# The coupling blocks of the 32x32 triangular inverses: from row operations on VectorE to 32x32 matrix products on TensorE

## The chip, the cores and the metric

The kernel runs on one core of a Trainium2 chip. A core has five engines that run side by side: TensorE (PE in the profile, with its weight loads listed as PEld), VectorE (DVE), ScalarE (ACT), GpSimd (POOL) and SyncE (SP), which here only issues DMA transfers. Each engine takes its instructions strictly in the order of its own queue and waits on semaphores for the others. The metric is the device time of one execution in microseconds (us), lower is better.

## The reference

One encoder layer over two sequences, 2048 and 512 tokens of width 1024: RMS norm, one input projection, four mixers of width 256 (a chunked gating MLP, a bidirectional gated DeltaNet, a grouped-query attention, a pooling mixer), each times a SiLU gate, then an output projection and the residual. All inputs and outputs are float32. The change touches the DeltaNet alone, and of it this part, once forward and once over the flipped sequence, for 4 heads:

```python
q, k, v, g, beta = (to_chunks(t) for t in (q, k, v, g, beta))
g = jnp.cumsum(g, axis=-1)
decay = jnp.exp(jnp.where(incl, g[..., :, None] - g[..., None, :], -jnp.inf))
k_beta = k * beta[..., None]
lower = jnp.where(strict, jnp.einsum("bnhid,bnhjd->bnhij", k_beta, k) * decay, 0.0)
eye = jnp.eye(DN_CHUNK, dtype=jnp.float32)
t_mat = lax.linalg.triangular_solve(lower + eye, jnp.broadcast_to(eye, lower.shape),
                                    left_side=True, lower=True, unit_diagonal=True)
u = t_mat @ v_beta
w = t_mat @ (k_beta * jnp.exp(g)[..., None])
# then a scan over the chunks: state -> (out, state), using w, u, q, k and t_mat's products
```

So for each chunk, head and direction a unit triangular matrix has to be inverted before the scan over the chunks may use it. The kernel uses chunks of 128 tokens, so that there are 20 of them (16 and 4), each with 4 heads and 2 directions: 160 matrices of 128x128.

## The kernel before, in words

The work is cut into five blocks of 512 tokens (four of the long sequence, one of the short one). A first phase computes the projection that the DeltaNet needs, its convolution and norms; a second one (`phase2`) computes, in three passes over the blocks, the other projections and gates; a third one (`phase3`) is the attention with the output projection mixed in. Products that must be accurate are made of three float16 products; they have 512 columns and stand at lines 127 and 135 (400 columns at line 400), 3000 in all. I call these the big products. Those of `phase2` are the filler beside which the DeltaNet runs.

`deltanet` runs at a higher priority than `phase2`'s second and third pass, and goes block by block, in the order 0, 3, 1, 2 and then the short sequence's block 4. For each block there are three steps and then the scan:

- `pre`, for each tile of 128 tokens: the decay and the products of the keys (`gp`, `kk` on TensorE, lines 1095 to 1110), the matrices `nl` (VectorE, line 1114) and the intra-chunk matrices. The four 32x32 diagonal blocks of each matrix go by DMA to the DRAM tensor `DG`, one matrix per row.
- `lanes`, once per block: `DG` comes back with one 32x32 block in each of the 128 partitions (`nf`), and each partition inverts its own block (`xf`) by elementwise products and sums along rows on VectorE. A helper `dot` does each step as a multiplication (line 1153) and a sum (line 1154). First the two 16x16 halves of the block are inverted together, 15 steps of growing length. Then the 16x16 block between the halves, `z`, is computed: four steps multiply by the matrix, four more by the second inverse. The result goes to the DRAM tensor `XL`.
- `levels`, for each pair of tiles, so twice per block: the inverses come back from `XL` with the blocks' rows across the partitions (`d32`, line 1179, four transfers per call). Products on TensorE couple 32x32 blocks to 64x64 (`z1p`, `t1p`, `tnp`, lines 1206 to 1217) and those to 128x128 (`z2p`, `t2p`). The first of these use 32x32 parts of the array, four at a time on different rows and columns. Between the products ScalarE moves results out of PSUM. The finished inverse goes as float16 pairs to DRAM.
- `rec` (lines 1256 to 1323), for each tile and direction: the scan itself, 40 steps, which load the finished inverses.

The order on each engine isn't written out: a list scheduler sets it when the program is built, from priorities (the DeltaNet's 3000000, the attention's 2000000, the later passes' 1000000) and its own estimate of when each instruction can run. A changed instruction therefore moves the rows of every engine after it. The tiles of the products in `levels` share two PSUM banks in turn (tag "CE").

## Time and profile before

| | |
|---|---|
| time, median of 3 runs | 1568.18 us (1568.1 to 1571.8) |
| the profiled execution's own time | 1574.01 us |
| its span, first to last instruction | 1572.2 us |
| mean granted TensorE clock | 0.959 |
| busy: PE, DVE, ACT, POOL | 1425.8, 1173.3, 797.0, 546.7 us |
| from the first to the last `z1p` product | 445.9 to 823.1 us |

The page lists busy times by engine, then the span in slices, then groups of instructions by line. "Idle before" is the time an engine stood still just before a group, and what ended it. The granted clock is the share of full speed that the chip let TensorE run at in a stretch. In a view of stretches each engine has its busy time and, in brackets, its number of instructions. Products of 512 columns overlap in TensorE, so the mean duration that the groups give for one is longer than the distance at which they follow each other. A float32 product stands in the trace as two records.

### The profile page before, as it was taken

How to read it: one execution, taken by the hardware profiler on the slowest of the kernel's cores; microseconds unless marked ns; L12 is line 12 of the kernel's file. 1: busy time of each engine (PE TensorE's matmuls, PEld its weight loads, DVE VectorE, ACT ScalarE, POOL GpSimd, SP SyncE). 2: the span in 40 equal slices, each digit the busy share in tenths (PEclk: the TensorE clock that was granted, in tenths of full speed). 3: DMA queues.
4: the chain of work that ended last, by engine and by line, in shares of the span. 5: the costliest groups of instructions: out<-in, count | busy, mean ns of one | idle time of the engine just before them, and what ended most of it. 6: DMA issues, size and time to landing. Idle time of an engine off the chain costs nothing. (4 is left out here: it accounts for less than half of the span.)

```text
span 1572.2 us, 34743 instructions
## 1 busy us (share of the span) xinstructions
PE 1425.8 (91%) x13420; PEld 783.5 (50%) x13420; DVE 1173.3 (75%) x2265; ACT 797.0 (51%) x1655; POOL 546.7 (35%) x646
## 2 busy tenths in 40 slices
PE   6999999988989887987889879998799999999898
PEld 3456555543444443544445435555355555555443
DVE  6338579967969887996957769998877887877611
ACT  5244444545454844554546215565567675576400
POOL 3220220044748643455453435555121221121100
PEclk9999999998899989989999999999799999999999
DMA  9845643556566877657689885644411501414332
GB/s 254 283 168 168 190 151 114 150 194 193 160 186 201 258 234 218 199 171 215 186 259 311 278 255 177 202 139 148 161 48 39 173 34 65 160 33 135 114 128 107
DMA packets 250830, 269.65 MB, mean 172 GB/s; under 512 B 95784, under 2 KB 176680, under 8 KB 250024
## 3 DMA queue, kind: packets, MB, share of 16 engines
q1 hardware_dynamic: 250264, 267.36, 54.1%
q8 instruction: 105, 1.72, 0.4%
q14 instruction: 61, 0.50, 0.1%
q0 software_dynamic: 400, 0.07, 0.1%
HBM read 175.66 MB, written 91.77 MB: 170 GB/s over the span
## 5 line engine op out<-in xcount | busy, mean ns | idle before, releaser
L127 PEld LDWEIGHTS <-w 128*128 128x128 f16 x2280 | 223.5, 101 | 307.5 <-issue 81.8
L127 PE MATMUL accz<-xs,w 128*128 128x512 f16 x960 | 243.7, 402 | 16.8 <-DMA xs<-xs 6.7
L958 PE MATMUL op<-wo,mx 128*128 128x512 f16 x960 | 225.3, 379 | 1.0 <-DVE y L962 1.0
L886 DVE TENSOR_REDUCE mm<-mp 128x1 f32<-128x512 f32 x272 | 179.5, 683 | 52.4 <-PE mp L884 52.1
L916 POOL TENSOR_TENSOR p<-e,p 128x512 f16<-128x512 f32 x68 | 86.7, 1274 | 318.6 <-ACT p L915 283.7
L912 ACT ACTIVATE e<-sp 128x512 f32<-128x512 f32 x272 | 153.4, 596 | 79.3 <-PE sp L910 72.9
L916 DVE TENSOR_TENSOR p<-e,p 128x512 f16<-128x512 f32 x204 | 165.8, 828 | 19.3 <-ACT p L915 19.1
L127 PE MATMUL acc<-xs,w 128*128 128x512 f16 x720 | 162.8, 383 | 3.8 <-POOL xs L291 1.5
L915 ACT ACTIVATE p<-e 128x512 f16<-128x512 f32 x272 | 161.2, 632 | 3.4 <-PE O L921 2.0
L921 PEld LDWEIGHTS <-p 128*128 128x128 f16 x3264 | 128.1, 97 | 55.8 <-DVE p L916 11.2
L921 PE MATMUL O<-vt,p 128*128 128x65 f16 (+1 forms) x3264 | 142.6, 193 | 7.5 <-DVE p L916 5.3
L958 PEld LDWEIGHTS <-mx 128*128 128x128 f16 x960 | 91.3, 98 | 104.4 <-issue 1.8
L884 PE MATMUL mp<-ka,qa 128*128 128x512 f16 x272 | 98.7, 395 | 17.3 <-DVE mm L886 10.6
L909 PE MATMUL sp<-qa,ka 128*128 128x512 f16 x272 | 103.9, 384 | 2.6 <-ACT e L912 1.2
L306 DVE SCALAR_TENSOR_TENSOR cv<-raw,convw,cv 128x512 f32<-128x512 f32 x120 | 88.0, 754 | 21.2 <-POOL raw L382 20.6
L910 PE MATMUL sp<-qb,kb 65*128 65x512 f16 x272 | 100.5, 387 | 1.2 <-ACT qb L894 1.0
L127 PE MATMUL accq<-xs,w 128*128 128x512 f16 x360 | 89.5, 391 | 9.9 <-DMA xs<-xs 7.0
L400 PE MATMUL acct<-wtm,xs 128*128 128x400 f16 x480 | 83.8, 332 | 1.9 <-ACT ba L408 0.9
L1268 POOL TENSOR_TENSOR kd<-kv,kds 128x512 f16<-128x512 f32 x40 | 46.9, 1179 | 108.0 <-PE up L1305 56.0
L291 POOL TENSOR_TENSOR xs<-xt,xs 128x512 f16<-128x512 f32 x36 | 49.1, 1386 | 73.5 <-ACT xs L288 73.2
L962 DVE SCALAR_TENSOR_TENSOR y<-op,xr 128x512 f32<-128x512 f32 x40 | 27.5, 687 | 59.2 <-PE op L958 59.1
L127 PE MATMUL accu<-xs,w 128*128 128x512 f16 x240 | 60.9, 403 | 7.2 <-DVE s L616 7.0
(316 smaller groups left out, 2506.8 us busy)
## 6 DMA issues: line engine op xcount, KB each, us to landing
xs<-xs SPq DMA_DIRECT2D x120, 256.0 KB
kx<-kx SPq DMA_DIRECT2D x80, 256.0 KB
at<-at SPq DMA_DIRECT2D x80, 256.0 KB
tt<-tt SPq DMA_DIRECT2D x80, 256.0 KB
xt<-in_xT SPq DMA_DIRECT2D x40, 256.0 KB
xs<-xs SPq DMA_DIRECT2D x5, 2048.0 KB
kv<-kv SPq DMA_DIRECT2D x40, 256.0 KB
mix<-mixs SPq DMA_DIRECT2D x40, 256.0 KB
```

Source lines behind the costliest of these rows:

```text
L127: mm = self.nc.tensor.matmul(ps, w[:, a, k, :], xk, start=k + i == 0, stop=k == 7 and i == 2)
L306: V.scalar_tensor_tensor(cv, raw[:, ct, i:i + 512], self.convw[:, ct, i:i + 1], cv, op0=ALU.mult, op1=ALU.add)
L400: PE.matmul(acc[:, 0:400], xs[:, a, k, tt * 128:(tt + 1) * 128], w[:, c, k, :], start=n == 0, stop=n == 23)
L884: PE.matmul(mp, qa[:, qt * 128:qt * 128 + 128], KA[h // 2][:, sc * 512:sc * 512 + 512], start=True, stop=True)
L886: V.tensor_reduce(mm[:, qt, sc:sc + 1], mp, axis=AX.X, op=ALU.max)
L909: PE.matmul(sp, KA[kv][:, c], qa, start=True, stop=False)
L910: PE.matmul(sp, KB[kv][:, c], qb, start=False, stop=True)
L912: A.activation(e, sp, AF.Exp)
L915: A.activation(p[:, 0], e, AF.Copy)
L916: (G if st % E8 == 1 else V).tensor_tensor(p[:, 1], e, p[:, 0], op=ALU.subtract)
L921: mm = PE.matmul(O[:, qt, 0:z - a], p[:, w, q], v[:, a:z], start=st == 0 and qt == 0 and i == 0, stop=st == nst - 1 and i == 2, skip_group ...
L958: PE.matmul(op, mix[k][:, a, tt * 128:tt * 128 + 128], wo[k][:, c, n * 512:n * 512 + 512], start=i + j == 0, stop=i == 7 and j == 2)
```

## The change

`lanes` now stops after the two 16x16 halves: the eight steps for `z` are gone, and with them the larger scratch tile. `levels` gets what was in `z` as a level of its own ahead of the others. It loads the inverses of both directions in one transfer (`d32s`, 64 rows of `XL`; `pre` writes the rows of `DG` in another order, so that these 64 rows are together). VectorE transposes all of them (`dT`). Then 64 products of 32x32 by 32x16 on TensorE (`zcp`: 8 matrices, 2 directions, 4 diagonal blocks, each block on its own part of the array's diagonal) multiply the matrices' 32x32 diagonal blocks with one column half of the inverses. ScalarE takes the results out of PSUM for each direction, scaled row by row by 0 or 1 (the new constant `m16`) to keep the rows of one half, into `zcs` and a part of `dT`. 64 more products (`ucp`) multiply with the other half, and VectorE adds the result to the upper right 16x16 quarters in `d32s`. From there the levels are as before. `levels` is called ten times, `lanes` five.

```diff
@@ late_consts @@
+        self.m16 = cp.tile([128, 2], F32, name="m16")
+        nc.sync.dma_start(self.m16, I["m16"])
@@ front @@
-        for x in TTs + Tns:
+        zcs = dp.tile([128, 8, 32], F32, name="zcs")
+        for x in TTs + Tns + [zcs]:
             G.memset(x, 0.0)
@@ pre @@
-                l0 = (t % 4 * 2 + d) * 16
+                l0 = t % 4 // 2 * 64 + d * 32 + t % 2 * 16
                 nc.sync.dma_start(self.DG[t // 4][l0:l0 + 16].rearrange("(u b) (r c) -> (b r) u c", u=4, r=32), dg)
@@ lanes @@
             def dot(out, x, y, shape):
-                tmp = dp.tile([128, 1024], F32, tag="ltmp", name="ltmp", bufs=1)
+                tmp = dp.tile([128, 450], F32, tag="ltmp", name="ltmp", bufs=1)
...
             for i in range(1, 16):
                 dot(xh[:, :, 0:i, i], xh[:, :, 0:i, 0:i], nh[:, :, i:i + 1, 0:i], [128, 2, i, i])
-            z = xt[:, 0:16, 16:32]
-            for k in range(0, 16, 4):
-                dot(z[:, k:k + 4, :], nl[:, 16:32, k:16].unsqueeze(1), xt[:, k:k + 4, k:16].unsqueeze(2), [128, 4, 16, 16 - k])
-            for k in range(12, -4, -4):
-                w = xt[:, 16:20 + k, 16 + k:20 + k].rearrange("p b a -> p a b")
-                dot(z[:, :, k:k + 4], w.unsqueeze(1), z[:, :, 0:k + 4].unsqueeze(2), [128, 16, 4, k + 4])
             nc.sync.dma_start(self.XL[b], xf[:, 0:1024])
@@ levels @@
+            l0 = t % 4 // 2 * 64
+            d32s = dp.tile([128, 2, 8, 32], F32, tag="d32", name="d32", bufs=1)
+            dT = dp.tile([128, 2, 8, 32], F32, tag="dT", name="dT", bufs=1)
+            flat = lambda x: x.rearrange("p d u r -> p (d u r)")
+            nc.sync.dma_start(d32s.rearrange("p d u r -> p (d u) r"),
+                              self.XL[t // 4][l0:l0 + 64].rearrange("(v b) (c r) -> (b c) v r", b=4, c=32))
+            V.transpose(flat(dT), flat(d32s))
+
+            blocks = [slice(B * 32, B * 32 + 32) for B in range(4)]
+            zcp = self.bank("CE", [128, 2, 8, 16], "zcp")
+            for u in range(8):
+                for d in both:
+                    for r in blocks:
+                        PE.matmul(zcp[r, d, u, :], at(d, u, r, r), d32s[r, 1, u, 16:32] if d else dT[r, 0, u, 0:16],
+                                  start=True, stop=True, tile_position=(r.start, r.start))
+            zc = dT[:, 0, :, 16:32]
+            A.activation(zcs[:, :, 0:16], zcp[:, 0], AF.Identity, scale=self.m16[:, 0:1])
+            A.activation(zc, zcp[:, 1], AF.Identity, scale=self.m16[:, 1:2])
+            ucp = self.bank("CE", [128, 2, 8, 16], "ucp")
+            for u in range(8):
+                for d in both:
+                    for r in blocks:
+                        PE.matmul(ucp[r, d, u, :], dT[r, 1, u, :] if d else zcs[r, u, :],
+                                  zc[r, u, :] if d else d32s[r, 0, u, 16:32], start=True, stop=True,
+                                  tile_position=(r.start, r.start))
+            V.tensor_tensor(d32s[:, :, :, 16:32], d32s[:, :, :, 16:32], ucp, op=ALU.add)
             for d in both:
                 TT, Tn = TTs[d], Tns[d]
-                d32 = dp.tile([128, 8, 32], F32, tag=f"d32{d}", name="d32", bufs=1)
-                for j in range(2):
-                    l0 = ((t + j) % 4 * 2 + d) * 16
-                    nc.sync.dma_start(d32[:, j * 4:j * 4 + 4], self.XL[t // 4][l0:l0 + 16].rearrange(
-                        "(u b) (c r) -> (b c) u r", u=4, c=32))
+                d32 = d32s[:, d]
                 if d == 0:
-                    tnd = dp.tile([128, 8, 32], F32, tag="tnd", name="tnd", bufs=1)
+                    tnd = dT[:, 0]
                     V.transpose(tnd.rearrange("p u r -> p (u r)"), d32.rearrange("p u r -> p (u r)"))
```

Lines of the changed kernel are numbered a little differently: 1184 is `zcp`, 1187 and 1188 the two moves out of PSUM, 1193 `ucp`, 1196 the addition, 1177 the new transposition; the steps of `dot` are at 1155 and 1156.

On VectorE, in the second block's `lanes`, the end of the old row operations looked like this (`ltmp` is the scratch tile, `lx` the inverse; the sums with 4x16 and 16x4 results belong to `z`; the other rows are `phase2`'s and the scan's):

```order
L1154 TENSOR_REDUCE lx<-ltmp 128x4x16
L660 SCALAR_TENSOR_TENSOR sg<-sh,pinv,rawp 64x512
L1153 TENSOR_TENSOR ltmp<-lnl,lx 128x256
L1154 TENSOR_REDUCE lx<-ltmp 128x4x16
L1153 TENSOR_TENSOR ltmp<-lx 128x1024
L1154 TENSOR_REDUCE lx<-ltmp 128x16x4
L1309 TENSOR_SCALAR S<-up 128x256
L1153 TENSOR_TENSOR ltmp<-lx 128x768
L723 TENSOR_TENSOR k<-k,rb 128x512
```

In the changed kernel VectorE's row after the last step of the halves (2x15) belongs to the levels of the block before, and the addition of `ucp` stands in the queue with the transpositions behind it:

```order
L1155 TENSOR_TENSOR ltmp<-lx,lnl 128x450
L1119 SCALAR_TENSOR_TENSOR dt<-kk,dt 128x256
L1156 TENSOR_REDUCE lx<-ltmp 128x2x15
L1262 TENSOR_TENSOR tt_5366<-tt_4485,tt_5366 128x1024
L725 TENSOR_TENSOR k<-k,rb 128x512
L1196 TENSOR_TENSOR d_5377<-d_5377,ucp 128x16x16
L1202 STREAM_TRANSPOSE dT<-d_5377 128x256
L1210 STREAM_TRANSPOSE tt_4486<-d_5377 32x8x32 x4
L1321 TENSOR_TENSOR v_5682<-up,v_5682 128x256
```

Sixteen row operations per block have left the queue, and two rows per call of `levels` have come in, the second of which waits for a product of TensorE.

On TensorE the first level of the first block began with `z1p`, right behind the big products of `phase2` (`accq`):

```order
L127 LDWEIGHTS w_1471
L127 MATMUL accq<-xs_4003,w_1471 128x512
L1206 MATMUL z1p<-tnd,nl 32x32
L1206 MATMUL z1p<-d_5119,nl 32x32
L1206 MATMUL z1p<-tnd,nl 32x32
```

Now it begins with `zcp`, and the scheduler lays products of the next block's `pre` (`kk`, line 1113) and of `phase2` (`rb`) in between:

```order
L1184 MATMUL zcp<-dT,nl 32x16 x4
L1184 MATMUL zcp<-d_5088,nl 32x16
L636 LDWEIGHTS rexp_3315
L636 MATMUL rb<-rt_3754,rexp_3315 128x512
L1184 MATMUL zcp<-d_5088,nl 32x16 x3
L1184 MATMUL zcp<-dT,nl 32x16 x4
L1184 MATMUL zcp<-d_5088,nl 32x16 x4
L1184 MATMUL zcp<-dT,nl 32x16 x4
L1184 MATMUL zcp<-d_5088,nl 32x16 x2
L1113 LDWEIGHTS kx
L1113 MATMUL kk<-kx 128x256
```

Counted over the whole order, 1605 of the 3000 big products stood ahead of the first `z1p` and 2541 ahead of the last level's last product; now 1488 stand ahead of the first `zcp` and 2230 ahead of that last product. The last step of the scan had 2991 of them ahead and has 2776 now. The products on 32x32 parts of the array stood in 46 runs without another product in between, and stand in 84.

More of the change, by code (lines that the diff above doesn't have):

```diff
@@ L1140, in lanes @@
             xf = dp.tile([128, 1056], F32, tag="lx", name="lx", bufs=1)
-            sq = lambda t: t[:, 0:1024].rearrange("p (a b) -> p a b", b=32)
             halves = lambda t: t.rearrange("p (h x) -> p h x", x=528)[:, :, 0:512].rearrange(
                 "p h (a b) -> p h a b", b=32)[:, :, :, 0:16]
-            nl, xt, nh, xh = sq(nf), sq(xf), halves(nf), halves(xf)
+            nh, xh = halves(nf), halves(xf)
             nc.sync.dma_start(nf[:, 0:1024], self.DG[b])
@@ L1458, in host_arrays @@
     out["rexp2"] = np.tile(blk[:, 4:6].T, (3, 1))
+    half = (np.arange(128) % 32 >= 16).astype(f4)
+    out["m16"] = np.stack([half, 1 - half], 1)
     out["sel"] = np.tile(np.eye(8, dtype=f4), (3, 1))
```

## The prediction

> **What bounds the kernel now.** I read the page's first part, then the stretches, cut at the first and the last `z1p` product and at the phases, then who waits for whom where TensorE loses time.
>
> ```profile
> PE 1425.8 (91%) x13420; PEld 783.5 (50%) x13420; DVE 1173.3 (75%) x2265; ACT 797.0 (51%) x1655; POOL 546.7 (35%) x646
> L1206 PE MATMUL z1p<-tnd,nl x320: 191/191/258, 445.9 to 823.1; 32*32 32x32 f32 x160
> core 0: us, PE busy (x) PEld busy (x) DVE busy (x) ACT busy (x) POOL busy (x), PEclk, DMA share, GB/s
> 360.00:446.00 86.00, 76.59 (x370) 34.60 (x373) 67.31 (x145) 43.75 (x113) 48.49 (x82) 0.88 0.65 199
> 446.00:823.00 377.00, 319.58 (x3969) 176.54 (x3972) 314.88 (x603) 204.26 (x472) 195.72 (x263) 0.91 0.69 210
> 823.00:1120.00 297.00, 258.47 (x3038) 147.27 (x3027) 242.32 (x430) 142.05 (x277) 142.42 (x140) 0.94 0.67 214
> 1120.00:1505.00 385.00, 373.69 (x3892) 211.78 (x3891) 293.87 (x514) 241.79 (x452) 74.88 (x56) 1.00 0.27 89
> ```
>
> Over the whole span TensorE is the busy engine, and from 1120 us on it is 97% busy at full clock (373.69 of 385). From 360 to 823 us it isn't: busy 396.2 of 463 us (76.59 + 319.58), and at a clock of 0.88 and 0.91. VectorE is busy 382.2 us there, 83%, ScalarE 54%. The time TensorE loses in these two stretches is 463 − 396.2 = 66.8 us of standing still and, at the granted clock, 86 x 0.12 + 377 x 0.09 = 44.2 us of slow running: 111 us. That is what can be won there, and nothing after 1120 us can.
>
> Whom TensorE waits for between the first and the last level:
>
> ```profile
> PE turned L626 <- POOL r L92: 11.2, 5, 3.5
> PE accu L127 <- DVE s L616: 7.0, 3, 4.2
> PE accq L127 <- DMA xs<-xs: 6.6, 7, 1.8
> PE gp L1095 <- DVE dt L1116: 6.2, 3, 3.8
> PE kk L1110 <- ACT dt L1102: 5.6, 3, 4.6
> PE accz L127 <- DVE k L723: 4.4, 1, 4.4
> PE up L1300 <- DMA tt<-tt: 3.4, 2, 2.5
> ```
>
> Of these 44.4 us, 17.6 end on VectorE itself and 11.2 on GpSimd's `r`, whose chain starts with a VectorE operation (line 66); 10.0 are DMA, 5.6 ScalarE. So 28.8 of 44.4, 65%, stand behind VectorE's queue. They are filler products that wait for a PSUM bank or a norm which VectorE has not come to yet.
>
> **What is removed.** The eight steps for `z`, five times: 40 multiplications and 40 sums.
>
> ```profile
> L1153 DVE TENSOR_TENSOR ltmp<-lx 128x1024 f32<-128x1024 f32 (+3 forms) x20 | 29.9, 1496 | 0.2
> L1153 DVE TENSOR_TENSOR ltmp<-lnl,lx 128x1024 f32<-128x1024 f32 (+3 forms) x20 | 19.0, 949 | 0.2
> L1154 DVE TENSOR_REDUCE lx<-ltmp 128x64 f32<-128x1024 f32 x10 | 12.1, 1213 | 0.2
> L1154 DVE TENSOR_REDUCE lx<-ltmp 128x64 f32<-128x768 f32 x10 | 9.5, 948 | 0.1
> L1154 DVE TENSOR_REDUCE lx<-ltmp 128x64 f32<-128x512 f32 x10 | 6.8, 680 | 0.2
> L1154 DVE TENSOR_REDUCE lx<-ltmp 128x64 f32<-128x256 f32 x10 | 4.1, 414 | 0.2
> ```
>
> 29.9 + 19.0 + 12.1 + 9.5 + 6.8 + 4.1 = 81.4 us of VectorE, all inside 360 to 823 us. Per block that is 16.3 us bare, but in the first block it spread over 33 us of wall time among other rows, from here:
>
> ```profile
> 397.54 1.22 DVE L1153 TENSOR_TENSOR ltmp<-lnl,lx 128x1024 f32<-128x1024 f32 x1
> 430.08 0.42 DVE L1154 TENSOR_REDUCE lx<-ltmp 128x64 f32<-128x256 f32 x1
> ```
>
> **What is added.** The nearest rows:
>
> ```profile
> L1183 DVE STREAM_TRANSPOSE tnd<-d 128x256 f32<-128x256 f32 x10 | 4.4, 439 | 10.2 <-DMA d<-xl 10.2
> L1302 DVE TENSOR_TENSOR v<-up,v 128x256 f16<-128x256 f32 x40 | 16.3, 416 | 3.4 <-ACT v L1301 3.4
> L1206 PE MATMUL z1p<-d,nl 32*32 32x32 f32 x320 | 9.3, 203 | 0.4 <-DMA d<-xl 0.3
> L1102 ACT ACTIVATE dt<-gp,lcj 128x128 f32<-128x128 f32 x160 | 44.7, 382 | 10.7 <-PE gp L1099 9.8 <-POOL at L1131 0.5
> core 0: us, PE busy (x), PEclk, DMA share, GB/s
> 440.00:448.00 8.00, 0.75 (x64) 1.00 0.97 252
> 630.00:650.00 20.00, 1.21 (x64) 0.91 0.62 179
> ```
>
> VectorE: a transposition of 128x512, twice the 128x256 one, 0.88 us, and an addition of 128x256 from PSUM, 0.42 us; ten times, 13.0 us. Net VectorE loses 81.4 − 13.0 = 68.4 us. ScalarE: two moves of 128x128 per call, 20 x 0.38 = 7.6 us, on an engine that is 54% busy; they cost the end nothing, and if ScalarE were full it would be those 7.6 us.
>
> TensorE: 20 bursts of 64 products. The last two rows are `z1p` alone, 32 products (64 records) of 32x32 by 32x32, four at a time: 0.75 us at full clock, 1.21 us at a clock of 0.91. The new ones have the same weights and half the columns. From below, if columns are all that counts, a burst is as long as one of `z1p`, 0.75 us; from above, twice the longer, 2.42 us. That makes 15 to 48 us. I take twice the shorter, 1.5 us, **30 us** in all, since the weights to load, one per product, don't get fewer. The Trainium skill, TensorEngine Tiling, Instruction Overhead, says that every matmul carries about 60 cycles, so that one column costs the same as sixty; by the 2.4 GHz of its page TensorE: Matmul & The Clock Gate I estimate from it 25 ns each, 32 us for the 1280. `z1p`'s 0.75 us for 32 products, 23 ns each, agrees in size.
>
> The transfers from `XL`: one per call instead of four, with the same 256 KB. VectorE waited 10.2 us in all for the four (the row of line 1183), TensorE 0.3 us (the row of line 1206): the filler covers the rest. Bounds −10 us, if none of it were waited for, and +10, if the one takes twice as long and the filler doesn't reach; I take 0. One memset and one constant's load stand before 360 us, off the path.
>
> New handoffs: TensorE, ScalarE, TensorE, VectorE, in each call. What queues behind the new addition on VectorE (line 1196) are the transpositions that `z1p` and `t1p` wait for, and then rows of the scan. The old rows for such waits are small: `kk` to `nl`, 80 times:
>
> ```profile
> L1114 DVE SCALAR_TENSOR_TENSOR nl<-kk,dt 128x256 f32<-128x256 f32 x80 | 32.3, 415 | 12.5 <-PE kk L1110 9.6 <-ACT dt L1102 2.7 <-PE z2p L1230 0.2
> ```
>
> 9.6 us for 80, 0.12 us each. 30 handoffs give 4 us; I take **3 us**. A level's chain gets longer by at least 0.88 + 1.5 + 0.76 + 1.5 + 0.42 = 5.1 us, 51 us over ten calls, against 81.4 us bare that leave the chain in `lanes`: it is shorter by 30 us before any queueing, and the order says the same, with 311 big products less ahead of the last level than before (2541 to 2230).
>
> **What the relief gives back.** This is the term that decides. 65% of 111 us is 72 us of TensorE's loss behind VectorE. VectorE's load in these two stretches goes from 382.2 of 463 us (83%) to 313.8 (68%), so its free share about doubles, 17% to 32%. If a wait behind a queue goes with the inverse of the free share, it falls to 0.53 of what it was, 34 us won. If VectorE paced the stretch outright, the stretch would shrink by 68.4 / 0.83 = 82 us. If only the 17.6 us of direct waits fell by half, it would be 9 us. Between 9 and 82 I take **47 us**, above the 34, because a standstill also brings a slow clock with it (in the slice from 425 to 436 us TensorE is held up and the clock falls):
>
> ```profile
> 425.00:436.00 11.00, 8.90 (x35) 3.53 (x35) 7.44 (x13) 3.41 (x10) 7.47 (x21) 0.69 0.72 237
> ```
>
> **Sum:** −47 + 30 + 3 = −14 us, on a span of 1572.2 us: 1558. The profiled execution took 1574.0 us by its own time and the median of the runs is 1568.2; 1568.2 − 14 = **1554 us**.
>
> **Rivals.**
>
> *TensorE's bursts cost more than VectorE's relief brings (slower).* The scan follows the levels at once: the order brings it forward too. VectorE's queue then stays as full as before between the levels, with rows of the scan in place of `z`, and TensorE keeps its waits while it has 20 bursts more. For it: what TensorE waits for are filler's banks and norms, all at lower priority than the DeltaNet, which stay behind whatever the DeltaNet gives VectorE. Against it: these rows are only moved, and are missing later, where VectorE is 82% busy as well (242.32 of 297). Price: relief 10, bursts 30 to 48, handoffs 3: +23 to +41, 1600 us. It decides as soon as the relief is under 33 us. The Trainium skill, TensorEngine Tiling, Key Properties, has a rule that pushes this way: a change of the tiling mode drains TensorE. The order has 38 runs more on 32x32 parts. What a change costs is read here:
>
> ```profile
> 448.58 3.40 PE L135 MATMUL accq<-xs,w 128*128 128x512 f16 x15
> 451.91 0.23 PE L1213 MATMUL t1p<-tt,z 32*32 32x32 f32 x4
> 1504.98 62.60 PE op L958 x290
> ```
>
> Big products follow each other at 62.60 / 290 = 0.216 us, so the last of the 15 started at 448.58 + 14 x 0.216 = 451.60, and the small ones 0.31 us after it: 0.1 us more than a big product's distance. 38 runs with a change at each end are 76 x 0.1 = 8 us by that row, within the 15 to 48. That rule, as a result of its own, is the sum with a drain in full: the 0.23 us of a small product for each change, 17 us, 1571 us; the trace's 0.1 us speaks against it.
>
> *No change.* The relief is about 33 us, by the inverse free share, and pays for bursts and handoffs exactly. 1568 us.
>
> *The chain was the bound (much faster).* VectorE paced the stretch: 82 us less, 30 + 3 more, 1519 us. For it: the whole wall of 33 us that `z` took in the first block. Against it: TensorE is 86% busy there, and after the change it would have to be over 95% busy from 360 to 823 us with its 30 us more; there isn't room for all of it.
>
> **How the numbers follow.** My forecast, 1534 to 1563 us: 0.46. Much faster, below 1534: 0.14. No change, within 0.3% (4.7 us, about what a measurement of this kernel can tell from none), the drain in full counted in here: 0.15. Slower: 0.25. Faster in sum 0.60. The range for 8 in 10 runs from the middle of the much faster case to near the slower one's price: **1526 to 1594 us**; the forecast's own is 1534 to 1563.
>
> **What would show it.** Right: in the stretch from 360 us to the last level, VectorE's share falls to about 70%, TensorE's goes to 90%, the clock rises above 0.93; `turned`, `accu` and `gp` wait less; a burst of `zcp` is 1.2 to 1.8 us; the last level ends 40 to 70 us earlier, and what remains runs as from 1120 us on now. Wrong: bursts over 2 us; new waits at line 1196 or of `ucp` for ScalarE above 0.5 us each; VectorE still above 80% in that stretch; or the earlier end of the levels lost again between them and 1120 us, where the filler that was moved behind them finds VectorE full.

## The result: 2.75% slower, and the profile after

The changed kernel takes 1614.07 us (median of 4 runs, 1604.62 to 1619.35) beside 1569.7 us for the kernel before (4 runs). The ratio is 1.0275, 95% interval 1.0220 to 1.0331. I had forecast 1554, faster. The profiled execution took 1619.35 us, its span is 1617.5 us, the mean granted clock 0.950 (before: 1572.2 and 0.959). Two executions of the experiments below stand far apart from the others of their kernels and are left out of the times, one of e3 (7165 us) and the profiled one of e4 (1823 us, at a granted clock of 0.748).

The first part of the page of the changed kernel:

```profile
PE 1454.6 (90%) x15980; PEld 816.4 (50%) x15980; DVE 1122.9 (69%) x2205; ACT 802.4 (50%) x1675; POOL 521.8 (32%) x647
```

Its stretch from 360 us to the last level product:

```profile
core 0: us, PE busy (x) PEld busy (x) DVE busy (x) ACT busy (x) POOL busy (x), PEclk, DMA share, GB/s
360.00:829.50 469.50, 392.42 (x7101) 229.81 (x7102) 323.15 (x710) 256.66 (x624) 231.07 (x337) 0.88 0.68 202
```

VectorE is relieved: 50.4 us less over the span, 69% of the stretch (323.15 of 469.5). TensorE is no busier for it, 84% (392.42 of 469.5) where I wanted 90%, at a clock of 0.88 where I wanted 0.93. First and last starts of four tiles' products say where the time went. Before:

```profile
L1236 PE MATMUL t2p<-tt,z x320: 218/218/363, 464.9 to 858.8; 64*64 64x64 f32 x160
L1305 PE MATMUL up<-v,kd x480: 189/193/258, 498.2 to 1098.7; 128*128 128x64 f16 x160
L127 PE MATMUL accz<-xs,w x960: 376/379/634, 317.3 to 1089.7; 128*128 128x512 f16 x192
L958 PE MATMUL op<-wo,mx x960: 376/379/390, 1132.0 to 1567.2; 128*128 128x512 f16 x192
```

After:

```profile
L1255 PE MATMUL t2p<-tt,z x320: 218/218/267, 451.0 to 829.6; 64*64 64x64 f32 x160
L1324 PE MATMUL up<-v,kd x480: 189/193/261, 469.3 to 1062.0; 128*128 128x64 f16 x160
L127 PE MATMUL accz<-xs,w x960: 376/379/634, 319.8 to 1159.9; 128*128 128x512 f16 x192
L960 PE MATMUL op<-wo,mx x960: 376/379/631, 1174.8 to 1612.7; 128*128 128x512 f16 x192
```

The levels (`t2p`) end 29 us earlier (I had said 40 to 70), the scan (`up`) 37 us earlier, but the filler (`accz`) ends 70 us later, and the output projection (`op`) starts 43 us later. From there to its last product it takes 435 us before and 438 us after. So nearly all of the 45 us of span is lost ahead of the output projection.

TensorE alone by stretches, the kernel before and then the changed one; the columns are the length, TensorE's busy time, the granted clock, the DMA share and GB/s:

```profile
360.00:600.00 240.00, 205.50 (x1947) 0.89 0.66 203
600.00:880.00 280.00, 240.73 (x2938) 0.93 0.73 227
880.00:1130.00 250.00, 217.12 (x2538) 0.94 0.62 196
```

```profile
360.00:600.00 240.00, 209.39 (x3252) 0.90 0.70 210
600.00:880.00 280.00, 214.49 (x4208) 0.83 0.68 205
880.00:1130.00 250.00, 226.73 (x2216) 0.98 0.62 198
```

I add up in each stretch what TensorE loses, as in the prediction: standing still (length less busy) and running slowly (length times what the clock lacks). From 360 to 600 us it loses 60.9 before and 54.6 after; from 600 to 880 us 58.9 and **113.1**; from 880 to 1130 us 47.9 and 28.3. In the first and the third stretch together it loses 26 us less, in the middle one 54 us more. The balance is 28 us of loss; the other 17 of the 45 us are near what 20 bursts last at full clock (1.26 us each, below, 25 us).

This sum is rough, since standing still at a slow clock counts in both terms. The trace also records each step of the clock. If every moment of TensorE's work is weighted with the clock granted at that moment, its work at full clock is 1371.7 us before and 1394.5 us after, 23 us more; the rest of the span, lost to standing still or to running slowly, is 200.5 us before and 223.0 us after, 22 us more. Together they are the 45 us.

Who is waited for tells what happened. The scan's four products before and after (the number behind the bar is busy time, then the mean, then idle time just before them):

```profile
L1300 PE MATMUL up<-r,tt 128*128 128x64 f16 x480 | 26.5, 200 | 11.5 <-DMA tt<-tt 3.4 <-ACT r L1295 2.7 <-DVE r L1296 2.3
L1288 PE MATMUL up<-s,kx 128*128 128x64 f16 x576 | 24.3, 193 | 2.1 <-ACT s L1283 1.3 <-DVE o L1314 0.5 <-DVE s L1284 0.3
L1305 PE MATMUL up<-v,kd 128*128 128x64 f16 x480 | 19.9, 194 | 0.1
L1312 PE MATMUL up<-v,at 128*128 128x64 f16 x480 | 19.9, 194 | 1.2 <-DVE S L1307 1.1 <-DVE S L1309 0.2
```

```profile
L1307 PE MATMUL up<-s,kx 128*128 128x64 f16 x576 | 27.8, 201 | 24.1 <-DVE o L1333 16.4 <-DVE zz L609 5.7 <-DVE s L1303 2.0
L1319 PE MATMUL up<-r,tt 128*128 128x64 f16 x480 | 26.8, 200 | 23.8 <-DMA tt<-tt 7.7 <-DVE r L1315 7.0 <-DVE o L1310 6.0
L1324 PE MATMUL up<-v,kd 128*128 128x64 f16 x480 | 22.6, 202 | 11.1 <-DVE v L1321 11.1
L1331 PE MATMUL up<-v,at 128*128 128x64 f16 x480 | 21.8, 198 | 9.2 <-DVE S L1326 7.7 <-issue 1.5
```

14.9 us before, 68.2 us after. Each step of the scan is a round trip, TensorE to VectorE and back; before, more of other products stood between one trip and the next, as counted below. The filler's waits went the other way. Its three groups of line 127 before and after:

```profile
L127 PE MATMUL accz<-xs,w 128*128 128x512 f16 x960 | 243.7, 402 | 16.8 <-DMA xs<-xs 6.7 <-DVE k L723 4.4 <-DVE gz L607 4.2
L127 PE MATMUL accq<-xs,w 128*128 128x512 f16 x360 | 89.5, 391 | 9.9 <-DMA xs<-xs 7.0 <-DVE q L708 1.7 <-ACT rawp L834 1.0
L127 PE MATMUL accu<-xs,w 128*128 128x512 f16 x240 | 60.9, 403 | 7.2 <-DVE s L616 7.0 <-DVE gz L607 0.2
```

```profile
L127 PE MATMUL accz<-xs,w 128*128 128x512 f16 x960 | 241.5, 399 | 6.7 <-DMA xs<-xs 4.0 <-ACT rawp L833 1.1 <-ACT rt L631 0.7
L127 PE MATMUL accq<-xs,w 128*128 128x512 f16 x360 | 93.3, 411 | 1.9 <-ACT rawp L836 1.0 <-DMA xs<-xs 0.9
L127 PE MATMUL accu<-xs,w 128*128 128x512 f16 x240 | 58.2, 390 | 0.9 <-DVE s L618 0.4 <-DVE zz L609 0.3 <-DVE gz L609 0.2
```

33.9 us before, 9.5 us after: the filler waits 24 us less, the scan 53 us more. That VectorE's relief is what the filler gained isn't shown: in e1 below, which has the relief and no new product, these three groups wait 31.2 us.

One place in the changed kernel's timeline shows the form of it (start, duration, instruction, and in brackets the idle time before it), and then TensorE in the stretches around it:

```profile
840.98 1.86 PE L1307 MATMUL up<-s,kx 128*128 128x64 f16 x32 [3.25 <-DVE o L1333]
851.27 1.01 PE L1307 MATMUL up<-s,kx 128*128 128x64 f16 x16
852.16 0.80 PE L1324 MATMUL up<-v,kd 128*128 128x64 f16 x12
852.58 1.76 DVE L1000 MEMSET kb<- 1x2048 f16 x1 [0.48 <-issue]
854.73 2.85 DVE L1000 MEMSET kb<- 1x2048 f16 x3 [0.38 <-DMA kv<-kv]
857.95 0.41 DVE L1326 SCALAR_TENSOR_TENSOR S<-up,S 128x256 f32<-128x256 f32 x1
858.41 0.80 PE L1331 MATMUL up<-v,at 128*128 128x64 f16 x12 [5.46 <-DVE S L1326]
863.00 0.59 PE L628 MATMUL turned<-id,r 128*12 128x128 f16 x4 [3.79 <-POOL r L92]
```

```profile
835.00:840.90 5.90, 2.73 (x34) 1.00 0.73 226
840.90:863.00 22.10, 7.70 (x120) 0.50 0.71 225
```

The state `S` needs the product that ends at 852.96. On VectorE it stands behind four settings of `kb`, which the attention's preparation queued there, 4.6 us of them; TensorE waits 5.46 us for it with nothing else in its queue ahead. In the 22 us from 840.9 us on TensorE works 7.70 us, and the clock is at 0.50. The Trainium skill, TensorE: Matmul & The Clock Gate, HAM oscillation — how this bites in real kernels, says that gaps of more than about 3.4 us halve the clock; the trace agrees on the half. On the length it agrees only roughly: the clock falls from 1.00 to 0.50 at the end of a wait of 3.25 us, and the gaps of 5.46 and 3.79 us lie in a stretch that is already slow.

### The profile page after: what moved, and what is told of

Read it like the earlier page. It is cut to its first block, busy times and chain, and to the rows that moved or that the text cites. A ratio compares the mean times of both kernels' runs of the same rounds, so it can differ in the third digit from the quotient of the medians.

```text
span 1617.5 us, 39812 instructions
## 1 busy us (share of the span) xinstructions
PE 1454.6 (90%) x15980; PEld 816.4 (50%) x15980; DVE 1122.9 (69%) x2205; ACT 802.4 (50%) x1675; POOL 521.8 (32%) x647
## 4 chain that ended last, share of the span: by engine, by line
PE 48%; DVE 21%; DMA 15%; ACT 5%; issue 5%; POOL 2%; SPq 2%; DVEq 0%; ACTq 0%; POOLq 0%
PE op L960 11%; PE accz L127 7%; PE O L923 5%; PE acc L127 3%; DVE cv L308 3%; PE sp L911 3%; PE sp L912 3%; PE accq L127 3%; PE mp L886 2%; DMA tt<-tt 2%; DVE p L918 2%; PE accq L135 2%; DMA xs<-xs 2%; PE acct L402 1%; PE accu L127 1%
## 5 line engine op out<-in xcount | busy, mean ns | idle before, releaser
L923 PE MATMUL O<-vt,p 128*128 128x65 f16 (+1 forms) x3264 | 138.5, 193 | 4.1 <-DVE p L918 3.9
L886 PE MATMUL mp<-ka,qa 128*128 128x512 f16 x272 | 92.3, 379 | 16.7 <-DVE mm L888 8.3
L127 PE MATMUL accq<-xs,w 128*128 128x512 f16 x360 | 93.3, 411 | 1.9 <-ACT rawp L836 1.0
L293 POOL TENSOR_TENSOR xs<-xt,xs 128x512 f16<-128x512 f32 x36 | 49.1, 1388 | 77.5 <-ACT xs L290 77.3
L1134 POOL TENSOR_TENSOR at<-dt,at 128x512 f16<-128x512 f32 x40 | 49.4, 1234 | 57.7 <-ACT at L1133 46.0
```

The lines of the kernel that those rows point to most:

```text
L127: mm = self.nc.tensor.matmul(ps, w[:, a, k, :], xk, start=k + i == 0, stop=k == 7 and i == 2)
L886: PE.matmul(mp, qa[:, qt * 128:qt * 128 + 128], KA[h // 2][:, sc * 512:sc * 512 + 512], start=True, stop=True)
L923: mm = PE.matmul(O[:, qt, 0:z - a], p[:, w, q], v[:, a:z], start=st == 0 and qt == 0 and i == 0, stop=st == nst - 1 and i == 2, skip_group ...
```

## Experiments

The theories, where an expectation has only a letter for them: P, the parts are what counts (relief of VectorE against new products); S, the scan, which stands bare between few other products in the changed order, makes the loss; O, the order of equal instructions as such is worth tens of us. "The kernel before" is run beside each; its medians were 1573 to 1576 us in these sessions, and the ratios go by it. One number is worked out from the order: how much work of other products TensorE has between two groups of scan products (products counted in the order, each by its distance in the trace, 0.216 us for a big one). It is an estimate: median 2.22 us and 24 of 115 groups with nothing between before, 0.76 us and 61 of 155 in the change.

### The parts alone

**e1**: `z` left out (the block between the halves is then not computed), nothing in its place; the merged load stays.

```diff
@@ before: lanes @@
-            z = xt[:, 0:16, 16:32]
-            for k in range(0, 16, 4):
-                dot(z[:, k:k + 4, :], ...)
-            for k in range(12, -4, -4):
...
-                dot(z[:, :, k:k + 4], ...)
@@ before: pre, levels @@
(the merged load, as in e3)
```

> The z steps are gone and nothing is put in their place (no transposition, no zcp and ucp, no addition; the coupling blocks stay zero, so the DeltaNet part of the result is left wrong); the merged load stays. Theory S (the scan is bared): with VectorE relieved, the scheduler brings the scan forward even without the new products, its products stand closer together in TensorE's queue (135 groups with 1.6 us of other work between them in the median, against 115 with 2.2 us before and 155 with 0.8 us in the change), so TensorE's waits ahead of the scan's products are 25 to 45 us (15 before, 68 in the change) and eat most of the 34 us that the filler's waits give back: 1555 to 1575 us. Theory P (the products themselves and their handoffs are the loss): the full relief is left, the scan's waits stay near 15 us, 1530 to 1545 us.

Measured: 1544.17 us, 0.9782 [0.9754, 0.9810]. The scan's products wait 14.8 us, so P's case holds and S's doesn't. The filler's three groups wait about as long as before, 31.2 us against 33.9:

```profile
L127 PE MATMUL accz<-xs,w 128*128 128x512 f16 x960 | 238.7, 398 | 17.9 <-DVE gz L609 5.7 <-DVE s L618 3.6 <-DMA xs<-xs 3.5
L127 PE MATMUL accq<-xs,w 128*128 128x512 f16 x360 | 86.4, 386 | 10.7 <-DMA xs<-xs 8.0 <-DVE q L710 1.5 <-ACT rawp L836 1.0
L127 PE MATMUL accu<-xs,w 128*128 128x512 f16 x240 | 58.8, 392 | 2.6 <-DVE s L618 1.7 <-DVE zz L609 0.8
```

**e3**: the kernel before with the merged load and the row order of `DG` alone.

```diff
@@ pre @@
-                l0 = (t % 4 * 2 + d) * 16
+                l0 = t % 4 // 2 * 64 + d * 32 + t % 2 * 16
@@ levels @@
+            d32s = dp.tile([128, 2, 8, 32], F32, tag="d32", name="d32", bufs=1)
+            nc.sync.dma_start(d32s.rearrange("p d u r -> p (d u) r"), self.XL[t // 4][l0:l0 + 64]...)
-                d32 = ... (four transfers per call)
+                d32 = d32s[:, d]
```

> The kernel before with nothing but the merged load and the other order of the rows of DG. No engine's work changes. Theory S: the order of the scan's products alone moves the time, since it has 154 groups with 1.3 us between them: scan waits 30 to 55 us, 1585 to 1605 us. Theory P: within 5 us of before, 1565 to 1575 us.

Measured: 1572.13 us, 0.9975 [0.9954, 0.9996]. The transfers are worth nothing, as forecast. The time is P's, and S is contradicted: the scan's products wait 32.8 us, which is within S's range, and the kernel isn't slower for it. Against e3, e1's relief is 28 us. Where it arrived, the waits say only in part. The products of `pre`, `gp` and `kk`, wait 12.1 us in e1, against 25.7 in e3 and 24.2 before. The scan waits 18 us less than in e3, but as long as before. The three groups of filler wait less than before and more than in e3 (25.4 us).

**e2**: `z` stays on VectorE and the new level's products and moves, two transpositions and an addition run as well, their result weighted by zero.

```diff
@@ e3: levels @@
+            (64 zcp products, two moves, 64 ucp products as in the change)
+            V.scalar_tensor_tensor(d32s[:, :, :, 16:32], ucp, 0.0, d32s[:, :, :, 16:32], op0=ALU.mult, op1=ALU.add)
```

> The z steps stay on VectorE, and the new level is added beside them: the load, two transpositions, 64 and 64 products, two moves, and an addition of zero times the products. VectorE is not relieved. Theory S: TensorE pays 29 us for the bursts, and the scan, with 143 groups and 1.3 us between them, waits 35 to 55 us: 1610 to 1640 us, the same as or above the change. Theory P: products and handoffs cost the whole 45 + 34 = 80 us: 1650 us.

Measured: 1603.62 us, 1.0171 [1.0141, 1.0201]. Against e3 the new level costs 31 us. That is below both theories' ranges; the scan waits 34.2 us.

**e5**: the changed kernel with products, moves and addition for four of the eight matrices (the other four lack the block).

```diff
-            for u in range(8):
+            for u in range(4):
```

> The change with the products, the moves and the addition for four of the eight matrices only (the others keep a coupling block of zero, so that part of the inverses is left wrong). Bursts cost TensorE 14 us instead of 29. Theory O (products cost their busy time once, the rest of the loss is the order in which the scan then stands): 1544 + 14 + 4 = 1562 us and what the order adds; it has 145 scan groups with 1.3 us of other work between them, between the bare one of the change (155, 0.8) and the kernel without products (135, 1.6): 1562 to 1580 us. Theory P (every product costs more than twice its busy time, whatever the order): half way between the kernel without products and the change, 1579 to 1585 us.

Measured: 1554.15 us, 0.9877 [0.9844, 0.9910], 8 us under O's range and 25 under P's.

**e6**: the changed kernel without the 1280 products; the transposition, two moves (from SBUF) and two additions stay (the block is then not computed).

```diff
-            (64 zcp products; the two moves out of zcp; 64 ucp products; the addition of ucp)
+            A.activation(zcs[:, :, 0:16], dT[:, 1, :, 0:16], AF.Identity, scale=self.m16[:, 0:1])
+            A.activation(zc, dT[:, 1, :, 16:32], AF.Identity, scale=self.m16[:, 1:2])
+            V.tensor_tensor(d32s[:, 0, :, 16:32], d32s[:, 0, :, 16:32], zcs[:, :, 0:16], op=ALU.add)
+            V.tensor_tensor(d32s[:, 1, :, 16:32], d32s[:, 1, :, 16:32], zc, op=ALU.add)
```

> The change without its 1280 products: the load, the transposition of 128x512, two moves on ScalarE (from SBUF) and the addition stay, so that the handoffs VectorE, ScalarE, VectorE are in the chain (the coupling blocks get other numbers and are left wrong). Both theories: 1544 us and 12 us of VectorE at the rate at which its relief pays (29 us of time for 81 us of VectorE), 4 us: 1545 to 1553 us. More than 1560 us would mean that the handoffs, not TensorE's busy time, carry the loss.

Measured: 1568.86 us, 0.9951 [0.9927, 0.9974]: a miss by 16 us for both theories, and slower than e5, which does more. So no sum of parts orders these kernels: 1544 for none of the new level, 1569 with its small rows and no products, 1554 with half of all.

### The same instructions in another order

e4, e9, e11, e15 and e17 change nothing but the order. `EARLY`, which e7, e10, e13, e14 and e16 lower, also sets the number of buffers of `nl`, 8 + 2 x `EARLY`, so these five have two or four buffers fewer.

**e4**: the changed kernel; the scan steps of a block are queued one block later. No instruction is added or taken away.

```diff
-            ready.add(b)
+            ready.update(order[:i] if i < len(order) - 1 else order)
```

> The change, with the scan's steps of each block queued one block later (the same instructions, another order). Its products stand 135 groups with 1.8 us of other work between them instead of 155 with 0.8 us. Theory S: the waits ahead of the scan's products fall from 68 to 25 to 40 us and the time to 1575 to 1595 us. Theory P: the waits of the scan were only a symptom, the time stays within 8 us of the change, 1606 to 1622 us.

Measured: 1582.79 us, 1.0042 [1.0020, 1.0064]: 31 us off the change by order alone, within S's range. **e8** is the same kernel once more, for its profile.

> The change with the scan's steps queued one block later, once more for its profile at full clock: 1575 to 1590 us. Theory O: the waits ahead of the scan's products are 25 to 40 us, against 68 in the change, and TensorE's standstill is 10 to 25 us less in all.

Measured: 1587.57 us in one run, 38.9 us of waits ahead of the scan's products. TensorE stands still for 142.9 us of the span, 20 us less than in the change.

**e7**: e4 with `EARLY = 3` (of the next block's four `pre`, this many are queued ahead of the first `levels`).

> The change with the scan's steps queued one block later, and three instead of four of the next block's tiles prepared ahead of the first levels. Same instructions; the scan's products stand as in the kernel before: 114 groups, 2.4 us of other work between them (115 and 2.2 before; 155 and 0.8 in the change; 135 and 1.8 with the later scan alone). Theory O: the loss by order is gone, and what is left is relief and bursts, 1570 to 1582 us, with scan waits of 15 to 25 us. Theory P: 1600 to 1620 us.

Measured: 1587.27 us, 1.0078 [1.0048, 1.0107]; its scan has as much other work between (2.39 us, 25 bare) as before, and still waits 42.9 us. O missed the time by 5 us and the waits by 18, and S doesn't explain it.

**e9**: the edit of e4 in the kernel before.

> The kernel before with one edit: the scan steps of a block are queued one block later, as in e4; no instruction is added or taken away. Theory P (the parts are what counts, and the order of equal instructions moves the time by 5 us or less): 1570 to 1580 us beside a kernel before at 1575. Theory O (the order alone is worth some 30 us in a kernel of this load): it differs from the kernel before by 10 us or more to either side; by the waits, the scan's products wait more than the 14.9 us of before, since the median work between them falls from 2.2 to 1.3 us of TensorE.

Measured: 1573.0 us, 1.0004 [0.9980, 1.0028], scan waits 23.9 us. The time is P's; the waits rose, as O had them.

**e10**: the changed kernel with `EARLY = 3`.

```diff
-EARLY = 4
+EARLY = 3
```

> The changed kernel with one number changed, EARLY from 4 to 3; again the same instructions in another order. The median TensorE work between two groups of scan products goes from 0.76 to 1.44 us, and 48 groups instead of 61 have nothing between them and the group before. Theory O: 1583 to 1600 us, faster than the change as it was made, with 35 to 55 us of waits ahead of the scan's products instead of 68. Theory P: 1605 to 1619 us, as the change.

Measured: 1577.78 us, 1.0020 [1.0001, 1.0039]. One number takes back 36 of the 44 us, and the time is 5 us under O's range. Its stretches:

```profile
360.00:600.00 240.00, 210.61 (x3278) 0.89 0.71 212
600.00:880.00 280.00, 229.11 (x4239) 0.90 0.73 217
880.00:1130.00 250.00, 234.22 (x2422) 0.98 0.63 197
```

Lost there: 55.8, 78.9 and 20.8 us. Against the change as built 34 of the 41 us less are in the middle stretch; the scan's waits are 43.0 us instead of 68.2.

**e11**: e6 with the edit of e4.

> e6 (the changed kernel without the 1280 small products and with its two moves and the additions left; the blocks between the halves are therefore not computed) with the scan steps queued one block later, as in e4. Theory O (e6 came out 20 us above its parts by its order): 1545 to 1560 us. If instead the transposition, the moves and the additions cost 20 us by themselves, wherever they stand: 1565 to 1573 us, as e6.

Measured: 1559.25 us, 0.9906 [0.9873, 0.9940]. In reach of O, at its upper end: the order takes 10 of e6's 16 us. It stays 15 us above e1, which lacks the small rows; whether these rows or another order cost that isn't shown.

**e12**: the kernel before with the 40 multiplications of `z` on GpSimd.

```diff
-                V.tensor_tensor(t, x.to_broadcast(shape), y.to_broadcast(shape), op=ALU.mult)
+                M.tensor_tensor(t, x.to_broadcast(shape), y.to_broadcast(shape), op=ALU.mult)   # M = GpSimd for z
```

> The kernel before with the 40 multiplications of z on GpSimd instead of VectorE (the 40 sums stay on VectorE); no product is added on TensorE. VectorE is freed of 49 us, GpSimd gets the 40 at about 2 us for 1024 elements a row (it takes 2.17 us for such a product elsewhere in the trace), some 65 us. In its order the scan stands as bare as in the change (median 0.71 us of other TensorE work between its groups, 65 groups with none). Parts alone: relief 49/81 of 29 us, so 1555 to 1562 us. If a bare scan costs what it seems to cost in the change: 1575 to 1590 us, with 50 us or more of waits ahead of the scan's products.

Measured: 1593.94 us, 1.0138 [1.0097, 1.0178], slower without a single product more. It doesn't tell the theories apart: the scan's waits are 41.9 us, under the 50 named, and the time is above the range. The 40 took 71.1 us on GpSimd, yet the levels don't come later: `z1p` runs from 443.3 to 792.3 us, before from 445.9 to 823.1. TensorE loses 86 us from 360 to 600 us, 25 more than before; why isn't shown.

### Is it the change or the order? The same rule with and without it

e10 left open whether the change has one unlucky order or orders scatter that widely for any kernel here. Four rules (e4's, `EARLY` 3, `EARLY` 2, and the scan's steps queued for two of the four scans at a time in every block) were therefore run on both sides.

**e13** is the kernel before with `EARLY` 3; **e16** is the kernel before with 2, and **e14** the change with 2:

```diff
-EARLY = 4
+EARLY = 3   (e13)
+EARLY = 2   (e14, e16)
```

**e15** and **e17**: the change and the kernel before with

```diff
-                for r in sorted(go, key=lambda r: -len(r))[:2] if i == len(order) - 1 else go:
+                for r in sorted(go, key=lambda r: -len(r))[:2]:
```

> The kernel before with EARLY from 4 to 3, as e10 is for the changed kernel. Its scan gets as bare as the change's (median 0.86 us of other TensorE work between its groups, 60 groups with none, against 2.22 us and 24). If a bare scan by itself costs the 36 us: 1595 to 1615 us, with 50 us or more of waits ahead of the scan's products. If the loss takes more than that (the place at which the scan meets other work on VectorE): within 10 us of the kernel before, 1565 to 1585 us.

> The changed kernel with EARLY at 2: median 1.30 us of other TensorE work between the scan's groups, 48 groups with none, as e10 has. If the order that the change was built with is an outlier: 1573 to 1590 us. If e10 was the outlier: 1600 to 1620 us. In the first case the loss of TensorE (standing still and slow clock) from 600 to 880 us is below 90 us, against the change's 113.

> The changed kernel with the scan's steps of every block queued for two of the four scans at a time, the longest first, as the last block has it already: the same instructions, median 0.94 us of other TensorE work between the scan's groups, 54 groups with none. If the order as built is an outlier: 1575 to 1595 us. If the bare scan sets the time: 1600 to 1615 us, between the change (0.76 us and 61) and e10 (1.44 us and 48).

> The kernel before with EARLY at 2, the pair of e14 (1614.6 us). If the change itself costs some 40 us and EARLY little: 1570 to 1580 us. If the change itself is worth within 10 us and the order makes the rest: the pair is as likely to come out on either side, and the kernel before lies between 1573 and 1615 us, the spread seen so far. Its scan is bare (median 0.85 us of other TensorE work between groups, as e13, which took 1606 us): by the bare scan 1600 to 1610 us.

> The kernel before with the scan's steps of every block queued for two of the four scans at a time, the pair of e15 (1593.4 us). Change worth some 40 us by itself: 1550 to 1560 us. Change worth within 10 us: 1575 to 1605 us. By the bare scan (median 1.08 us, as e9 with 1.29 us took 1573 us and e13 with 0.86 us 1606 us): 1580 to 1600 us.

Measured, each as median and ratio to the kernel before, with the waits ahead of the scan's products in us:

| rule for the order | without the change | scan waits | with the change | scan waits | difference |
|---|---|---|---|---|---|
| as built | 1569.7, 1 | 14.9 | 1614.1, 1.0275 [1.0220, 1.0331] | 68.2 | +2.8% |
| scan a block later (e9, e4) | 1573.0, 1.0004 [0.9980, 1.0028] | 23.9 | 1582.8, 1.0042 [1.0020, 1.0064] | 38.9 (e8) | +0.4% |
| `EARLY` 3 (e13, e10) | 1606.3, 1.0202 [1.0174, 1.0230] | 41.6 | 1577.8, 1.0020 [1.0001, 1.0039] | 43.0 | −1.8% |
| `EARLY` 2 (e16, e14) | 1618.4, 1.0288 [1.0264, 1.0312] | 49.2 | 1614.6, 1.0246 [1.0219, 1.0273] | 49.0 | −0.4% |
| two scans at a time (e17, e15) | 1570.3, 0.9980 [0.9961, 0.9998] | 19.2 | 1593.4, 1.0114 [1.0083, 1.0145] | 46.3 | +1.3% |

Of the expectations, e15's holds for an outlying order, and e13's time is that of a bare scan, though its waits are 41.6 us and not 50. e14 took the time that it was to have if e10 was the outlier, while its loss from 600 to 880 us, 84.8 us, is that of the other case. e16 lies above all its ranges, and e17 between them.

The kernel before loses as much to `EARLY` 2 (45 us in e16) as it lost to the change. Its stretches there:

```profile
360.00:600.00 240.00, 198.12 (x1864) 0.90 0.63 193
600.00:880.00 280.00, 233.99 (x2451) 0.92 0.71 222
880.00:1130.00 250.00, 200.44 (x2743) 0.86 0.64 197
```

Lost: 65.9, 68.4 and 84.6 us, 218.9 in all against 167.7, so 51 us more, 37 of them behind 880 us, where the levels of the last blocks now run: the last `t2p` starts at 944.3 us, before at 858.8. Its scan waits for the same kind of rows:

```profile
L1300 PE MATMUL up<-r,tt 128*128 128x64 f16 x480 | 27.6, 205 | 22.2 <-DVE o L1291 8.9 <-ACT r L1295 6.4 <-DVE r L1296 3.0
L1288 PE MATMUL up<-s,kx 128*128 128x64 f16 x576 | 27.9, 204 | 11.7 <-DVE zz L607 5.9 <-DVE o L1314 2.6 <-DVE s L1284 1.0
```

What follows. First, the mean of the five differences is +0.45%, 7 us; they scatter with a standard deviation of 1.7%, so the mean is uncertain by 12 us (one standard error). By the times alone the change can't be told from no change, nor from the −14 us of my sum. Its cost on TensorE can. Weighted by the clock as above, TensorE has 1367 to 1373 us of work in the profiles of the five kernels without the change and 1388 to 1397 us in the five with it (e8's for e4), 23 us more in the mean. The order hardly moves this. What it moves is the rest of the span, the lost time: in the order of the table's rows 200, 201, 223, 248 and 194 us without the change and 223, 198, 183, 217 and 192 us with it. The means, 213 and 203 us, are too close for such a scatter to show a relief.

Second, the order as built decided the sign: among these five the kernel before has a good one and the change a bad one. How much of that is luck isn't shown. In the three pairs with `EARLY` 4 the change is slower each time. In the two with 3 and 2 it is faster, but there the kernel before gets its last `t2p` at 923.5 and 944.3 us instead of 858.8, and in e16 VectorE waits 12.5 us to write `nl` until `z2p` has read a buffer (0.2 us before). So a lead of 4 suits the kernel before, and these two pairs change more than the order of equal work.

Third, within each side of the table the time rises with the waits ahead of the scan's products: without the change from 14.9–23.9 us (1570 to 1573) to 41.6 (1606) and 49.2 (1618); with it from 38.9–43.0 (1578 to 1583) over 46.3 (1593) to 49.0 and 68.2 (1615, 1614), so not in proportion. Other runs don't follow it: e3 waits 32.8 us at the time of the kernel before, e11 waits more than e6 (25.1 and 22.3 us) and is 10 us faster, and e7 and e10 wait alike (42.9 and 43.0 us) and are 9 us apart. The scan's waits are the largest group of TensorE's waits in the change as built; that they set the time of an order isn't shown.

What stays open is what in an order makes TensorE lose time, at the scan or elsewhere. How much other work TensorE has between the scan's groups isn't enough: without the change 1.08 us or more went with a good time and 0.85 and 0.86 us with a bad one, but with it e14 (1.30 us, 48 bare groups) took 1615 us and e10 (1.44 us, 48) 1578. The same scatter is in e1, e2, e5 and e6, each measured in one order, so that 28 and 31 us are known no better than the pairs' difference is. No version tried beats both kernels while it computes everything: e17 and e9 are at the time before, e10 too.

## Why the prediction was wrong

**What bounds the kernel now**: held. The stretch from 360 us is where all was won and lost, nothing behind the start of `op`.

**TensorE's bursts, 30 us (15 to 48)**: held. The 1280 products, by the two lines that issue them, and one burst of 64 (128 records). First line 1184, then line 1193, both over all their calls, then line 1184 in one call; the second pair of numbers is the weight loads:

```profile
360.00:1130.00 770.00, 16.81 (x1280) 14.15 (x1280) 0.90 0.67 204
360.00:1130.00 770.00, 16.98 (x1280) 14.32 (x1280) 0.90 0.67 204
452.00:454.00 2.00, 1.26 (x128) 1.16 (x128) 1.00 1.00 386
```

33.8 us busy at a mean clock of 0.90, 1.26 us for a burst at full clock (forecast 1.2 to 1.8; 20 ns a product, where the estimate had 25), 31 us in e2 against e3, and 23 us of work at full clock over the five pairs. One reading behind the upper bound was wrong: the `z1p` products of the 1.21 us ran from 635 to 637 us, at a clock of 1.00, and 0.91 is the mean of the row's 20 us. They took longer for another reason than the clock.

**VectorE, ScalarE, handoffs, transfers**: the rows held. The added rows are 7.1, 4.1 and 3.8 + 3.7 us:

```profile
L1177 DVE STREAM_TRANSPOSE dT<-d 128x512 f32<-128x512 f32 x10 | 7.1, 706 | 18.6 <-DMA d<-xl 18.6
L1196 DVE TENSOR_TENSOR d<-d,ucp 128x256 f32<-128x256 f32 x10 | 4.1, 411 | 0.2 <-PE ucp L1193 0.2
L1187 ACT ACTIVATE zcs<-zcp,m 128x128 f32<-128x128 f32 x10 | 3.8, 376 | 6.0 <-PE zcp L1184 5.9
L1188 ACT ACTIVATE dT<-zcp,m 128x128 f32<-128x128 f32 x10 | 3.7, 374 | 0.0
```

I had 13.0 us for VectorE (11.2), 7.6 for ScalarE (7.5). The addition waits 0.2 us in all, so this handoff costs VectorE's queue nothing; what all of them cost the end isn't shown (e11 against e1). The merged transfer is waited for 8.4 us longer than the four (18.6 against 10.2), inside my ±10, and e3 puts its price on the end at nothing.

**The relief, 47 us (9 to 82)**: mis-sized. The inverse of the free share had given 34; I raised it for the slow clock that a standstill brings, with one row that shows this and none that sizes it. Alone the relief measured 28 us (e1 against e3, one order each). With that the sum is +5 us, "no change", and not −14. Of the waits that I had named, those of `turned`, `accu` and `gp` got shorter in e1 (11.2 to 3.3, 7.2 to 2.6 and 16.5 to 9.0 us against the kernel before), those of `accz` and of line 127's `accq` didn't (16.8 and 17.9, 9.9 and 10.7 us).

**The sum itself failed**, and this is the larger error: it let TensorE's lost time follow VectorE's load alone. I counted the order's shift as rows that "are only moved" and gave it no term. With −47 and +3 the lost time was to shrink by 44 us; in the change as built it grew by 22, beside 23 us of new work where I had 30. A new order by itself takes back 31 us of the change (e4) and 21 us (e15), and `EARLY` 3 takes back 36 (e10); the kernel before can be moved by 45 us (e16, with four buffers fewer). A forecast from parts should have had a term of 0 for the order with bounds of some ±35 us, and its range should have been that much wider: 1614 lies outside mine.

**The rival on the slower side** was nearest in time, 1600 us, and right that the scan comes forward with the levels; its mechanism fell. It let VectorE's queue stay full and TensorE keep its old waits. VectorE emptied to 69%, the filler's waits fell from 33.9 to 9.5 us, and new waits came ahead of the scan, which the order now puts ahead of much of the filler. The sign I had named last under "wrong", the earlier end of the levels lost again behind them, came true for another reason: the moved filler doesn't find VectorE full, and the new waits stand at the scan. **Drain in full** (1571) isn't supported: with all their changes of tiling the bursts cost 31 us in e2 and 23 us of work over the pairs, where this rival had 47. **The chain was the bound** (1519) is refuted by e1, which shortens the chain and adds no product: 28 us, not 82.

## What to carry to other kernels

Where a scheduler sets the order, an edit is two changes: its own cost, and a new draw of the order. Measure how far the order alone moves the time (one priority or lead changed, no instruction) before believing a difference of that size, and compare edits in several orders each. Part the busiest engine's span into work at full clock and lost time: here the work was steady within 9 us over the orders of one side and showed the 23 us of new products, which the times alone couldn't. When a chain of round trips is sped up, look at what used to fill its gaps: relief on one engine may be worth only what the other can put there.

## What was not expected

- The change of one lead number, with not one instruction more or less (and two buffers fewer), made the kernel before 30 us slower (e13) and the changed one 36 us faster (e10).
- Less work wasn't less time: e6, without the 1280 products, took 1569 us, e5 with half of them 1554, and the same small rows as e6 in another order (e11) 1559.
- Multiplications moved from VectorE to the less busy GpSimd made the kernel slower in the one order tried (e12, +1.4%): 1.9 us each for the second four steps' products, where VectorE took 1.5 us.
